# The opening of a two-layer mixer kernel: sum of squares on TensorE, one scaling instruction, earlier modulation loads, weight splits on GpSimd

## The chip, the cores and the metric

The kernel runs on one core of a Trainium2 chip. The metric is device time in microseconds (us) for one execution of the whole program; lower is better. The engines are called by the names of the profile: PE is TensorE's matrix product, PEld its weight load, DVE is VectorE, ACT is ScalarE, POOL is GpSimd, SP is SyncE, which issues the DMAs.

## What is computed

Two layers over 1024 latent tokens and 256 context tokens, each 1024 wide. The opening of the first layer is what the change touches:

```python
shift, scale, gate = jnp.split(jax.nn.silu(c) @ w_mod + b_mod, 3, axis=-1)
shift_c, scale_c, gate_c = jnp.split(jax.nn.silu(c_ctx) @ w_mod + b_mod, 3, axis=-1)
h = rms_norm(x, g_pre) * (1 + scale[:, None, :]) + shift[:, None, :]
hc = rms_norm(xc, g_pre) * (1 + scale_c) + shift_c
z = split_cols(h @ w_in)
zc = split_cols(hc @ w_in)
```

`rms_norm` divides by the root of the mean square over the 1024 channels and multiplies by a vector. The rest of the layer is four token mixers (pooling, latent attention, differential attention, windowed attention), gates, a merge and an output projection. All of it is float32.

## The kernel before

Tokens lie in the free dimension and channels in the partitions, so a chunk of 512 tokens is eight tiles (k = 0 to 7) of 128 x 512. There are three chunks: 0 and 1 are the latent tokens, 2 is the context (256 wide). To keep float32 accuracy on TensorE, each operand is split into a high half and a low half (`split`, line 66: ScalarE rounds to the high half, another engine subtracts), and one product becomes three instructions (`mm3`, lines 76 to 78).

`startup` (line 360) is the opening. Three weight tiles are applied to chunk 0 while it is being normalised: for each k, nine products (three tiles by three) go into three banks of PSUM. This is called group k here. What stands before and around it:

- `fetch` (line 376) loads x in four DMAs of 512 KB for a chunk. `st.load` (line 270) loads one weight tile of 512 KB (384 KB for the one of 96 columns) into `wraw`, of which there are two buffers, and splits it; in the opening the low half is made by VectorE (`nc.vector`), and by GpSimd elsewhere (the default). `mod_load` (line 408) loads two tiles of 512 KB of modulation weights, `wmod` (3 buffers) and `wmr` (6 buffers).
- `scaled` (line 384) is the norm of a chunk: `sum_sq` squares tile by tile on ScalarE and adds on VectorE or GpSimd, `col_rs` (line 232) sums over the partitions by products with a column of ones on TensorE, scales on VectorE and takes the power -1/2 on GpSimd; `spread` (line 247) makes a row for all partitions from that, by four diagonals on VectorE and four products on TensorE. For chunk 0 the row is copied to SBUF (`rbs`) and GpSimd multiplies it into the eight tiles.
- `mod_rows(k)` and `mod_run(k)` compute shift for the 128 channels of tile k on TensorE (line 422, a transpose at 430), and `scale_dot(k, i)` computes scale by a dot over 1024 elements on VectorE (line 150); i = 0 is for the latent tokens, i = 1 for the context. `silu_row(i)` makes the row that the dots use, by `spread`.
- `finish(k, ...)` applies scale and shift to tile k and makes its two halves. For chunk 0 that is two ScalarE passes and a VectorE subtraction, for the other chunks a VectorE instruction (line 56), a ScalarE pass and another VectorE instruction.

A planner reorders instructions between the program and the queues of the engines, by an estimate of when each is ready; the written order is its priority. Each queue then runs in order. The DMAs all go through SP's queue. When chunk 0 is through, `startup` finishes chunks 1 and 2, and their products follow with the same three weights.

Two buffers matter for the change: `h_tile(1, 1)`, 128 x 8 x 512, holds the low halves of chunk 1 and is not used until then, and the PSUM tiles `pt` (two) hold what `spread` returns.

Of the kernel before, what the change touches and what calls it, by code (L numbers as in the profile page):

```python
# [8 lines left out]
F = mybir.dt.float32  # L9
# [7 lines left out]
D = 1024  # L17
# [15 lines left out]
def kernel(ctx: ExitStack, tc: tile.TileContext, A: dict, out: bass.AP):  # L33
# [326 lines left out]
    def startup(es, three, crow):  # L360
# [10 lines left out]
        h_tile(1, 0)  # L371

# [9 lines left out]
        rbs = {}  # L382

# [10 lines left out]
        def finish(k, c0, n):  # L394
            c = 0 if c0 < SEQ else 1
            x, hi, lo = X(k, c0), H(0, k, c0, n), H(1, k, c0, n)
            a, b = m0.ab[:, 1, k, c:c + 1], m0.ab[:, 0, k, c:c + 1]
            if c0:
                stt(x, x, a, rbs[c0], ALU.mult, ALU.mult)
                act(hi, x, AF.Identity, bias=b)  # L400
                stt(lo, x, b, hi.bitcast(F), ALU.add, ALU.subtract)
            else:
                act(x, x, AF.Identity, scale=a, bias=b)
                split(x, hi, lo)
# [3 lines left out]
        def mod_load(k):  # L408
            if k < KT:
                mw[k] = p.tile([128, KT, 128], F, name="wmod", tag="wmod", bufs=3)  # L410
# [27 lines left out]
        fetch(*ALL[0])  # L438
        st.load((0, three[0]), None, nc.vector)
        mod_load(0)  # L440
        st.load((0, three[1]), None, nc.vector)
        mod_load(1)
        st.load((0, three[2]), tiles, nc.vector)
        mod_load(2)
        def silu_row(c):
            for g in range(2):
                act(crow[c][:, g * 512:g * 512 + 512], spread(cs[:, 4 * g:4 * g + 4, c], 512, p, sq1))
        silu_row(0)
        side = scaled(*ALL[0])
        next(side)  # L450
        mod_rows(0)
        next(side)
        mod_run(0)
        mod_rows(1)
        next(side)
        row = p.tile([128, 512], F, name="rbs", tag="nacc")
        act(row, rbs[0])
        for k in range(KT):
            x = X(k, 0)
            tt(x, x, row, ALU.mult, nc.gpsimd)  # L460
        big = ps_s.tile([128, 1536], F, name="pss", tag="pss")
        for k in range(KT):
            mod_load(k + 3)
            mod_run(k + 1)
            mod_rows(k + 2)
            finish(k, *ALL[0])
            for i, t in enumerate(three):
                m = 96 if t == W_X else 128
                st.group((0, t), big[0:m, i * 512:i * 512 + 512], 0, 512, [k])
            if k == 1:  # L470
                silu_row(1)
            if k > 1 and k < 8 - WMB + 2:
                scale_dot(k - 2, 1)
            if k < 4:
                fetch(*ALL[1], [2 * k])
            if k == 4:
# [1181 lines left out]
```

## Time and profile before

| what | us |
| --- | --- |
| median of 3 runs | 2758.21 (2756.69 to 2758.29) |
| the profiled execution, its own time | 2752.67 |
| its span in the trace | 2750.5 |
| TensorE busy in the span | 2615.1 (95%) |
| VectorE busy | 1539.2 (56%) |
| ScalarE busy | 1185.3 (43%) |
| GpSimd busy | 810.2 (29%) |
| mean granted TensorE clock | 0.977 |

A busy TensorE is not one at its peak, since ends of products are modelled and overlap; the granted clock tells which of its two levels (1.2 and 2.4 GHz) a stretch had. Times in the rows are counted from the start of the span.

### The profile page before, as it was taken

The page shows a single profiled execution, that of the slowest core. Times are in us where ns is not written, and L with a number is a line of the kernel's source. Part 1 is how long each engine was busy: PE and PEld are TensorE (multiplying, and loading weights), DVE is VectorE, ACT ScalarE, POOL GpSimd, SP SyncE. Part 2 cuts the span into 40 slices and gives each one's busy share as a digit, 9 for nine tenths or more (in the row PEclk, how much of TensorE's full clock was granted, in tenths as well). Part 3 has the DMA queues.
Part 4 walks back from the last instruction along what each step waited for, and adds up shares of the span by engine and source line. Part 5 has one row for each costly group of instructions (what it writes and reads, how often), then busy time and mean ns, then how long its engine had stood idle before and what let it go on. Part 6 is the DMA issues. An engine that isn't in the chain of part 4 may idle for free.

```text
span 2750.5 us, 38390 instructions
## 1 busy us (share of the span) xinstructions
PE 2615.1 (95%) x14194; PEld 2208.5 (80%) x14194; DVE 1539.2 (56%) x2638; ACT 1185.3 (43%) x2176; POOL 810.2 (29%) x492
## 2 busy tenths in 40 slices
PE   7998998999999989999998998989999999999998
PEld 5777877788988878888877776877888888888878
DVE  7544788967654893322148553889866632233133
ACT  4433765666662211222245343776656722222231
POOL 4223434300002223433324313445100022444334
PEclk9999999999999999999999999999999999999999
DMA  6366324323434652221135276434423343222122
GB/s 237 104 196 203 121 81 136 120 85 95 116 120 138 200 165 73 76 75 61 35 104 192 85 204 195 139 100 132 118 72 111 88 131 104 79 85 88 48 77 100
DMA packets 209069, 322.27 MB, mean 117 GB/s; under 512 B 26740, under 2 KB 123634, under 8 KB 208882
## 3 DMA queue, kind: packets, MB, share of 16 engines
q1 hardware_dynamic: 208882, 319.83, 37.4%
q8 instruction: 111, 1.82, 0.3%
q14 instruction: 76, 0.62, 0.1%
HBM read 239.07 MB, written 77.86 MB: 115 GB/s over the span
## 4 chain that ended last, share of the span: by engine, by line
PE 72%; DVE 14%; DMA 4%; issue 4%; ACT 3%; POOL 2%; SPq 1%; POOLq 0%; DVEq 0%; ACTq 0%
PE pd L76 14%; PE pd L78 14%; PE pd L77 14%; PE acc L1018 6%; PE pt L1002 5%; PE pss L1113 2%; PE pt L76 2%; PE pt L77 2%; PE pt L78 2%; DVE P L974 2%; DVE mjunk L150 2%; PE pss L1171 1%; PE pss L1072 1%; DVE t L53 1%; PE pss L1074 1%
## 5 line engine op out<-in xcount | busy, mean ns | idle before, releaser
L76 PE MATMUL pd<-h,wh 128*128 128x512 f32 (+2 forms) x2288 | 859.2, 376 | 22.2 <-ACT sg L50 10.5
L78 PE MATMUL pd<-h,wl 128*128 128x512 f32 (+2 forms) x2288 | 846.0, 370 | 0.2 <-POOL wl L53 0.2
L77 PE MATMUL pd<-h,wh 128*128 128x512 f32 (+2 forms) x2288 | 845.4, 370 | 0.2 <-DVE h L56 0.2
L53 POOL TENSOR_TENSOR wl<-wraw,wh 128x1024 fp32r<-128x1024 f32 x106 | 260.2, 2455 | 1009.8 <-ACT wh L50 801.7
L76 PEld LDWEIGHTS pd<-h,wh 128*128 128x128 f32 (+1 forms) x2288 | 437.7, 191 | 87.7 <-ACT sg L50 11.3
L78 PEld LDWEIGHTS pd<-h,wl 128*128 128x128 f32 (+1 forms) x2288 | 436.7, 191 | 68.9 <-issue 1.5
L77 PEld LDWEIGHTS pd<-h,wh 128*128 128x128 f32 (+1 forms) x2288 | 437.8, 191 | 60.1 <-DVE h L56 1.0
L974 DVE CUSTOM_DVE_ANT_0 P<-pss,zero 128x1280 f32<-128x1280 f32 (+1 forms) x216 | 295.6, 1369 | 118.1 <-PE pss L1113 60.4
L53 DVE TENSOR_TENSOR tl<-pt,th 128x512 fp32r<-128x512 f32 (+1 forms) x420 | 276.8, 671 | 114.0 <-ACT th L50 110.8
L50 ACT ACTIVATE th<-pt 128x512 fp32r<-128x512 f32 (+1 forms) x420 | 241.0, 583 | 182.3 <-PE pt L1002 174.9
L53 DVE TENSOR_TENSOR sg<-sg,pt 128x512 f32<-128x512 f32 x96 | 65.4, 686 | 394.7 <-PE pt L78 394.7
L1002 PE MATMUL pt<-kc,P 128*128 128x128 f32 x1632 | 255.8, 277 | 14.4 <-DVE P L56 8.8
L1018 PE MATMUL acc<-th,vt 128*128 128x256 f32 x816 | 245.3, 314 | 6.3 <-ACT th L50 5.8
L1018 PE MATMUL acc<-tl,vt 128*128 128x256 f32 x816 | 220.2, 290 | 6.5 <-DVE tl L53 6.5
L50 ACT ACTIVATE wh<-wraw 128x1024 fp32r<-128x1024 f32 x124 | 130.6, 1053 | 201.8 <-PE pd L77 153.7
L1002 PEld LDWEIGHTS pt<-kc,P 128*128 128x128 f32 x1632 | 193.7, 142 | 25.1 <-DVE P L56 13.8
L50 ACT ACTIVATE sg<-pd 128x512 f32<-128x512 f32 x128 | 75.7, 591 | 318.7 <-PE pd L78 312.4
L50 ACT ACTIVATE P<-P,m 128x1280 f32<-128x1280 f32 (+1 forms) x144 | 182.8, 1269 | 69.8 <-DVE m L974 67.7
L53 POOL TENSOR_TENSOR m<-m,sg 128x512 f32<-128x512 f32 x96 | 131.4, 1375 | 197.6 <-DVE sg L53 196.3
L1018 PEld LDWEIGHTS acc<-th,vt 128*128 128x128 f32 x816 | 156.5, 192 | 37.2 <-ACT th L50 23.4
L1018 PEld LDWEIGHTS acc<-tl,vt 128*128 128x128 f32 x816 | 156.9, 192 | 19.7 <-DVE tl L53 12.8
L50 ACT ACTIVATE P<-P,negm 128x1280 f32<-128x1280 f32 (+3 forms) x144 | 146.6, 1018 | 31.3 <-DVE negm L974 30.4
(290 smaller groups left out, 3950.6 us busy)
## 6 DMA issues: line engine op xcount, KB each, us to landing
wraw<-in_w_in_dram SPq DMA_DIRECT2D x108, 512.0 KB, 3.5
wmt<-in_w_modt_dram SPq DMA_DIRECT2D x64, 256.0 KB, 2.9
wraw<-in_w_out_dram SPq DMA_DIRECT2D x32, 512.0 KB, 3.3
yd<-ot SPq DMA_DIRECT2D x108, 128.0 KB, 1.9
kt<-dkd SPq DMA_DIRECT2D x64, 160.0 KB, 3.2
qt<-dqd SPq DMA_DIRECT2D x72, 128.0 KB, 2.8
ya<-yd SPq DMA_DIRECT2D x36, 256.0 KB, 3.0
yb<-yd SPq DMA_DIRECT2D x36, 256.0 KB, 3.0
```

Of the source, the lines that this page charges most:

```text
L50: return nc.scalar.activation(out=o, in_=i, func=func, **kw)
L53: return (e or nc.vector).tensor_tensor(out=o, in0=a, in1=b, op=op)
L76: nc.tensor.matmul(ps, wh(k), xh(k), start=k == 0, stop=False)
L77: nc.tensor.matmul(ps, wh(k), xl(k), start=False, stop=False)
L78: nc.tensor.matmul(ps, wl(k), xh(k), start=False, stop=k == n - 1)
L150: nc.vector.tensor_tensor_reduce(out=jk, in0=a, in1=b, scale=1.0, scalar=start, op0=ALU.mult, op1=ALU.add, accum_out=o)
L974: nc.vector.tensor_tensor_reduce(out=o, in0=i, in1=zero.to_broadcast([128, nk]) if mask is None else mask, scale=-1.0, scalar=1e30 if h is ...
L1002: t = nc.tensor.transpose(pt[:, 2 * j + i, :], Ps[i][:, (g + j) * 128:(g + j + 1) * 128], ident)
L1018: nc.tensor.matmul(acc, vt[:, kts[g + j], :], x[:, j, :], start=g + j == 0 and a == 0, stop=g + j == nk - 1 and a == 1)
L1072: nc.tensor.matmul(o, qt[0:96, 0, qs], kh[0:96, ks], start=True, stop=False)
L1074: nc.tensor.matmul(o, qt[0:96, 1, qs], kh[0:96, ks], start=False, stop=True)
L1113: last["s"] = nc.tensor.matmul(ps[:, b0 - k0:b0 - k0 + n], qt[:, mp, qs], kv[mp][:, b0:b0 + n], start=True, stop=True)
```

## The change

Five things are changed in `startup`:

- The sum of squares of chunk 0 is no longer added up tile by tile. `first_rs` squares each tile on ScalarE and sums it over the partitions on TensorE at once: four products of one column for each of eight tiles, 32 in all. One VectorE reduction adds the eight partial sums; scaling and power follow as before.
- `finish` for chunk 0 takes the form of the other chunks: one VectorE instruction multiplies x by scale and by the spread row, which stays in PSUM. The copy `rbs` and GpSimd's eight products go.
- Modulation loads 0 to 5 are issued before the loop, load 0 ahead of the first weight tile. Loads 3 to 6 get their `wmod` from the memory of `h_tile(1, 1)`. Loads 6 and 7 follow at k = 1 and 2, and after them, at k = 2, all of chunks 1 and 2 of x.
- The low halves of the three weight tiles are made by GpSimd (the default of `st.load`).
- `silu_row(1)` and the first two dots of the context move to k = 0 and 1, and `finish(k)` moves ahead of `mod_run(k + 1)` and `mod_rows(k + 2)`.

```diff
+        spare = h_tile(1, 1, F).rearrange("p k n -> p (k n)").rearrange("p (s k n) -> p s k n", s=4, k=KT)
...
+        def first_rs():
+            pc = ps_o.tile([128, 512], F, name="acc", tag="acc")
+            for k in range(KT):
+                q = p.tile([128, 512], F, name="sq", tag="sq", bufs=3)
+                act(q, X(k, 0), AF.Square)
+                for i in range(4):
+                    nc.tensor.matmul(pc[:, 4 * k + i:4 * k + i + 1], q[:, i * 128:(i + 1) * 128], ones[:, 0:1],
+                                     start=True, stop=True)
+            rs = p.tile([128, 4], F, name="crs", tag="crs")
+            nc.vector.tensor_reduce(out=rs, in_=pc[:, 0:32].rearrange("p (k i) -> p i k", i=4), axis=AX.X, op=ALU.add)
+            ts(rs, rs, 1.0 / D, EPS, ALU.mult, ALU.add)
+            tt(rs, rs, nhalf[:, 0:4], ALU.pow, nc.gpsimd)
+            return rs
...
-            if c0:
-                stt(x, x, a, rbs[c0], ALU.mult, ALU.mult)
-                act(hi, x, AF.Identity, bias=b)
-                stt(lo, x, b, hi.bitcast(F), ALU.add, ALU.subtract)
-            else:
-                act(x, x, AF.Identity, scale=a, bias=b)
-                split(x, hi, lo)
+            stt(x, x, a, rbs[c0], ALU.mult, ALU.mult)
+            act(hi, x, AF.Identity, bias=b)
+            stt(lo, x, b, hi.bitcast(F), ALU.add, ALU.subtract)
...
-                mw[k] = p.tile([128, KT, 128], F, name="wmod", tag="wmod", bufs=3)
+                own = k < 3 or k == 7
+                mw[k] = p.tile([128, KT, 128], F, name="wmod", tag="wmod", bufs=3) if own else spare[:, k - 3]
...
-        fetch(*ALL[0])
-        st.load((0, three[0]), None, nc.vector)
-        mod_load(0)
-        st.load((0, three[1]), None, nc.vector)
-        mod_load(1)
-        st.load((0, three[2]), tiles, nc.vector)
-        mod_load(2)
...
+        fetch(*ALL[0])
+        mod_load(0)
+        st.load((0, three[0]))
+        mod_load(1)
+        st.load((0, three[1]))
+        mod_load(2)
+        st.load((0, three[2]), tiles)
+        for k in range(3, 6):
+            mod_load(k)
         silu_row(0)
-        side = scaled(*ALL[0])
-        next(side)
+        rs0 = first_rs()
         mod_rows(0)
-        next(side)
+        mod_rows(1)
+        rbs[0] = spread(rs0, 512, p, sq1)
         mod_run(0)
-        mod_rows(1)
-        next(side)
-        row = p.tile([128, 512], F, name="rbs", tag="nacc")
-        act(row, rbs[0])
-        for k in range(KT):
-            x = X(k, 0)
-            tt(x, x, row, ALU.mult, nc.gpsimd)
         big = ps_s.tile([128, 1536], F, name="pss", tag="pss")
         for k in range(KT):
-            mod_load(k + 3)
+            if k in (1, 2):
+                mod_load(k + 5)
+            finish(k, *ALL[0])
             mod_run(k + 1)
             mod_rows(k + 2)
-            finish(k, *ALL[0])
             for i, t in enumerate(three):
                 m = 96 if t == W_X else 128
                 st.group((0, t), big[0:m, i * 512:i * 512 + 512], 0, 512, [k])
+            if k == 0:
+                silu_row(1)
+                scale_dot(0, 1)
             if k == 1:
-                silu_row(1)
-            if k > 1 and k < 8 - WMB + 2:
-                scale_dot(k - 2, 1)
-            if k < 4:
-                fetch(*ALL[1], [2 * k])
-            if k == 4:
+                scale_dot(1, 1)
+            if k == 2:
+                fetch(*ALL[1])
                 fetch(*ALL[2])
                 side = scaled(*ALL[1], nc.gpsimd)
```

## Rows read from the trace of the kernel before

**Rows 1.** The page: busy time, share of the span and instructions of each engine.

```profile
PE 2615.1 (95%) x14194; PEld 2208.5 (80%) x14194; DVE 1539.2 (56%) x2638; ACT 1185.3 (43%) x2176; POOL 810.2 (29%) x492
```

**Rows 2.** Busy time in windows of 5 us; columns as the first line says.

```profile
core 0: us, PE busy (x) PEld busy (x) DVE busy (x) ACT busy (x) POOL busy (x), PEclk, DMA share, GB/s
10.00:15.00 5.00, 2.27 (x11) 1.96 (x11) 2.33 (x4) 2.58 (x4) 0.00 (x0) 1.00 1.06 390
...
35.00:40.00 5.00, 5.00 (x29) 3.24 (x29) 3.40 (x10) 2.44 (x5) 0.00 (x0) 1.00 0.95 333
```

**Rows 3.** Timeline, 5 to 33 us: start, duration, engine, line, what, count, [idle before].

```profile
5.35 0.63 ACT L50 ACTIVATE nacc<-h 128x512 f32<-128x512 f32 x1 [2.29 <-DMA h<-in_xt_dram]
8.32 2.08 PE L254 MATMUL pt<-dg,sq 128*128 128x128 f32 x8 [2.54 <-DVE dg L62]
13.13 1.86 PE L236 MATMUL acc<-ones,nacc 128*128 128x1 f32 x8 [2.73 <-DVE nacc L53]
14.92 3.57 PE L422 MATMUL pd<-wmod,cs 128*2 128x128 f32 x16
15.03 0.16 DVE L64 TENSOR_SCALAR crs<-acc 128x4 f32<-128x4 f32 x1 [1.96 <-PE acc L236]
15.11 1.23 DVE L53 TENSOR_TENSOR wl<-wraw,wh 128x1024 fp32r<-128x1024 f32 x1
15.27 1.95 POOL L53 TENSOR_TENSOR crs<-crs,nhalf 128x4 f32<-128x4 f32 x1 [14.34 <-DMA wmod<-in_w_mods_dram]
20.41 1.16 PE L254 MATMUL pt<-dg,sq 128*128 128x128 f32 x8 [0.38 <-DVE dg L62]
20.74 12.06 POOL L53 TENSOR_TENSOR h<-h,rbs 128x512 f32<-128x512 f32 x8 [3.52 <-ACT rbs L50]
```

**Rows 4.** The same timeline around group 0, and the last product of group 7.

```profile
29.55 0.50 PE L76 MATMUL pss<-h,wh 128*128 128x512 f32 x1
29.83 1.04 ACT L50 ACTIVATE w<-wraw 128x1024 fp32r<-128x1024 f32 x1
31.92 1.97 DVE L53 TENSOR_TENSOR w<-wraw,w 128x1024 fp32r<-128x1024 f32 x1
31.95 1.91 PE L422 MATMUL pd<-wmod,cs 128*2 128x128 f32 x16
33.94 0.50 PE L78 MATMUL pss<-h,w 128*128 128x512 f32 x1
...
65.50 0.63 PE L78 MATMUL pss<-h,w 128*128 128x512 f32 x1
```

**Rows 5.** The same timeline: VectorE's dots, and its scaling by the row in PSUM.

```profile
42.95 1.21 DVE L150 CUSTOM_DVE_ANT_0 jk<-wmr,z 128x1024 f32<-128x1024 f32 x1
44.40 2.12 DVE L150 CUSTOM_DVE_ANT_0 jk<-wmr,z 128x1024 f32<-128x1024 f32 x1
...
75.09 2.06 DVE L56 SCALAR_TENSOR_TENSOR h<-h,ab,pt 128x512 f32<-128x512 f32 x3
```

**Rows 6.** Timeline and windows (columns as rows 2) in a run of one-column products.

```profile
89.11 2.27 PE L549 MATMUL pss<-ones,n 128*128 128x1 f32 x16
...
89.27:90.30 1.03, 1.03 (x13) 1.03 (x11) 0.00 (x0) 0.00 (x0) 0.00 (x0) 1.00 0.00 0
90.30:91.38 1.08, 1.08 (x7) 1.08 (x7) 0.00 (x0) 0.00 (x0) 0.00 (x0) 0.52 0.00 0
```

**Rows 7.** GpSimd's splits (count, sum, mean ns); SP's waits; weight loads on the page.

```profile
L53 POOL TENSOR_TENSOR wl<-wraw,wh 128x1024 fp32r<-128x1024 f32 x4 | 9.6, 2394 | 27.3 <-ACT wh L50 27.3
...
SPq L72 <- DVE wl L53: 5.6, 1, 5.6
...
wraw<-in_w_in_dram SPq DMA_DIRECT2D x108, 512.0 KB, 3.5
```

**Rows 8.** Timeline: chunk 1's last load, and its first scaled tiles.

```profile
41.25 0.43 SPq L72 DMA_DIRECT2D h<-in_xt_dram  x1
...
68.01 2.05 DVE L56 SCALAR_TENSOR_TENSOR h<-h,ab,pt 128x512 f32<-128x512 f32 x3
```

## The prediction

> **What bounds the kernel now.** I read the head of the page first: TensorE is busy for 95% of the 2750.5 us span [rows 1]. An edit to the opening can only pay where TensorE is not yet fed, so next came busy time in slices of 5 us: from 10 to 15 us TensorE works 2.27 us of five, from 35 us on all of them [rows 2]. The timeline of the first 21 us shows why: a single chain. The squares of the first chunk (ScalarE, about 0.63 us each, from 5.35 us) are added up by VectorE. Four column sums on TensorE follow (eight instructions at 13.13), then the scaling (15.03), the power on GpSimd (15.27, 1.95 us) and the spread of the result. From 20.74 GpSimd multiplies eight tiles, 12.06 us in all [rows 3].
>
> The first product of the projection starts at 29.55, but the start that counts is later. The third weight's low half is made by VectorE from 31.92 to 33.89, and the last three products of group 0 wait for it until 33.94. The last product of group 7 starts at 65.50 [rows 4]: (65.50 - 33.94) / 7 = 4.51 us a group. TensorE needs for one group nine products of 512 columns (0.21 us each at 2.4 GHz, the higher of its two levels), one run of modulation rows (sixteen instructions, 1.91 us [rows 4]) and a transpose with its gaps: some 4.2 us. So from group 1 on TensorE is nearly the bound, and only an earlier 33.94 pays.
>
> The written order is not the order of execution. The first modulation rows stand before the column sums in the program and run after them [rows 3]: a planner orders each engine's queue by its own estimate of readiness. I must infer that order for the new kernel.
>
> **Removed, and off the path.** Gone are seven VectorE additions, eight GpSimd products and, from each group, one of two ScalarE passes. VectorE gets one instruction more per group, in the form of line 56 with the spread row in PSUM (2.06 us for three, 0.69 each [rows 5]). Per group VectorE then has two of these, 1.38 us, a dot of 1.21 us [rows 5] and three small ones of about 0.5 us together: 3.1 us. TensorE's 4.2 us hide that; without that cover the added one would cost 8 x 0.69 = 5.5 us, and a dot beside GpSimd work can take 2.12 us [rows 5]. I count nothing for it, nor for moving silu_row(1): its spread was ready early and filled a wait at 20.41 [rows 3], and it can fill the wait before group 0 ends again; if not, its sixteen instructions cost TensorE twice the 1.16 us of that row.
>
> **Added: 32 column sums on TensorE.** Each is two weight loads of 128 columns and two products of one column, so 64 instructions stand where eight stood. Eight took 1.86 us at 13.13, though the clock column reads 1.00 [rows 2, 3]. Sixteen of the same form took 2.27 us at 89.11, and in the stretch of it with the granted clock at 1.00 thirteen instructions begin in 1.03 us [rows 6]. So the opening runs at the lower of TensorE's two levels (1.2 GHz) whatever the column says. The modulation rows agree (sixteen in 3.57 us at 14.92, 1.91 us at 31.95), and the spreads (eight in 2.08 us at 8.32, 1.16 at 20.41): the rise falls between 15 and 20 us, while the engine was in that run of 128-column products [rows 3, 4].
>
> By 3.57 / 16 the lower level costs 64 x 0.22 = 14.1 us; by 0.1 each the higher costs 6.4. Which holds? At 89.11 TensorE goes through one-column products without a gap, and the granted clock falls from 1.00 to 0.52 in the middle of them [rows 6]. A stream of this form did not hold the higher level, so I take it that it does not bring it either: 14.1 us. The squares come faster (0.63 us a tile, against 1.76 us of sums).
>
> The first square is done at 5.98; the second half of the first silu row (2.08 us at 8.32 [rows 3]) is still to run on TensorE. End of the sums: 5.98 + 2.0 + 14.1 = 22.1 us, against 13.13 + 1.86 = 14.99 before.
>
> The Trainium skill ("TensorE: Matmul & The Clock Gate", Part 1: The HAM clock gate) puts this the other way for unbroken work: "the default state is throttled, and activity releases the throttle". The trace agrees for the modulation rows, where the clock rose; whether one-column products are such activity decides between the two prices, and the fall after 89 us speaks against it. That reading is the first rival below.
>
> **The queue behind it.** The scaling takes 0.16 us [rows 3]. The reduction has no row: it reads 32 columns from PSUM, so it lies between nothing beyond that scaling and the 0.69 us of a 512-column instruction [rows 5]; I take 0.2, the nearer in size. Power on GpSimd, 1.95 us: 22.5 to 24.5. The weight splits are now in the same GpSimd queue, 2.39 us each [rows 7], and 1.8 for the 96-column one by its size; on VectorE they took 1.23 to 1.97 [rows 3, 4]. In the old order VectorE took the scaling (15.03) ahead of the first split (15.11) [rows 3], and now a further 1 MB of modulation weights is loaded ahead of that first weight. So I expect the planner to queue the power first and the splits behind it.
>
> The first split then runs from 24.5 to 26.9. The raw weights have two buffers, and the third load on SP waits for the first split, as it did before (5.6 us of wait on the VectorE split [rows 7]); now it is issued at 26.9, with modulation loads 3 to 7 stuck behind it, and chunk 1's loads behind those. To landing 3.5 us [rows 7] gives 30.4, the high half on ScalarE 1.04 us [rows 4] gives 31.4, the low half 33.8. Group 0 ends its wait at 33.8, against 33.9.
>
> The scaled tile itself is ready earlier: spread at 26.2 (behind modulation rows 0 on TensorE, 22.1 to 25.7), VectorE 0.7, ScalarE 0.7, and some hops: about 28.3, against 29.55 [rows 4]. If the planner puts the first split ahead of the power, this path decides. Nine products after 28.3 end by 30.5, modulation rows 2 (1.91) may stand between, and group 1 starts near 32 instead of 34: -2 us.
>
> **Chunk 1.** Its four loads now stand behind modulation load 7, which waits for the second dot with the context's silu row; before, three were out earlier and the last was issued at 41.25 [rows 8], landed near 45. From 26.9, the third weight (0.5 MB), modulation loads 3 to 7 (5.2 MB) and chunk 1 (2.1 MB) take 20 us at 390 GB/s [rows 2], so they land by 47. The first scaled tile of chunk 1 was at 68.01 [rows 8], after eight squares, GpSimd's sums and one more spread. A later start of the sums costs up to 2 us, and a first chunk without stalls (4.2 for 4.51 us a group, seven times) gives 2 back. I count zero, with +-2.
>
> **Sum.** Between -0.1 (power first) and -2 (split first), with chunk 1's +-2: I take -1.0 us. The profiled execution took 2752.67 us (2750.5 of span, 2.2 around it) and would take 2751.7; the runs' median is 5.5 above it, so 2757.2.
>
> **Rivals.**
> - *The clock rises during the sums.* At 0.1 us each they keep pace with the squares and end near 13. Power to 15.3, first split to 17.7, third weight issued 17.7, landed 21.2, split by 24.7: group 0 is through 9 us earlier, chunk 1's loads move up with it, and most of it, -8, passes on: 2750 (2749 to 2753). For: TensorE would work without a gap from 6 us on, as it did before the rise near 18. Against: the fall after 89 us [rows 6].
> - *GpSimd's queue becomes the bound, through one interleaving.* Modulation rows 0 need the first load behind x, which lands while the sums run. If the planner puts those sixteen instructions ahead of the last sums, the sums end 3.6 us later, at 25.7, and everything behind the power moves along: third weight split at 37.4, group 0 through +3.5 us later; splits and chunk 1's sums on GpSimd then stretch two or three of VectorE's dots by 0.9 us each [rows 5], +2: 2763 (2760 to 2766). It decides from the point where the last column sum ends after 22.2 us. For: the rows stand first among what is ready. Against: the old order, where the sums went first [rows 3].
>
> **How the numbers follow.** Forecast 0.50, earlier clock 0.32, interleaving 0.18. Two tenths of a per cent, about what a measurement of this kernel can tell from no change, are 5.5 us: faster needs under 2752.7, slower over 2763.7. Nearly all of the first rival lies below that, and a little of the forecast: faster 0.32. Of the second somewhat under half lies above, and a few points are for costs that I bounded too low: slower 0.14. Same 0.54. The range is 2749 to 2763, with both rivals' middles in or at it; the forecast's own is 2753.5 to 2760.
>
> **What would show it.** Right: 64 one-column instructions about 0.22 us apart from 6 to near 22 us; the power on GpSimd near 22.5; SP waiting some 10 us on a GpSimd split before the third weight; the last products of group 0 at 33 to 34; the first chunk's last product at 64 to 66. Wrong: instructions 0.1 us apart before 15 us, the third weight issued before 20, group 1 starting before 28 (first rival); modulation rows among the column sums and group 0 ending after 36 (second). It also falls if chunk 1's first scaled tile, and not group 0, sets the difference.

## The result, and the profile after

The changed kernel takes 2774.93 us (median of 4 runs, 2769.65 to 2777.11) against 2757.46 for the kernel before on the same chip (4 runs, 2756.69 to 2758.29): ratio 1.0058, 95% interval 1.0039 to 1.0077. It is slower by 17.5 us, outside the predicted range. The profiled execution of after took 2775.81 us, 23 more than that of before, whose own time lay some 5 us under its median. So places in the opening are compared below between traces, and totals by medians only.

If the j-th product (lines 76 to 78) from the end of one trace is set against the j-th from the end of the other, after is 12.2 us late where group 0 ends, 13 to 16 through groups 1 to 6, 17.4 where group 7 ends, 21.3 at chunk 1's start, up to 27 within chunk 1 and 22.8 at 108 us. From there to the end it is mostly 22 to 24 (21 to 27 at the extremes, 23 at the end). In this pair of traces all of the loss lies in the first 110 us, in two places. TensorE's share on the page is again 95%, with 18.9 us more of busy time than in [rows 1]:

```profile
PE 2634.0 (95%) x14250; PEld 2225.1 (80%) x14250; DVE 1532.8 (55%) x2637; ACT 1180.8 (43%) x2167; POOL 805.7 (29%) x487
```

The timeline of after from 6 to 29 us, all engines (columns as [rows 3]; line numbers are those of the changed file, where the column sums of chunk 0 are L391 and the modulation rows L434):

```profile
6.04 5.28 PE L391 MATMUL acc<-ones,sq 128*128 128x1 f32 x24 [0.32 <-ACT sq L50]
...
13.02 8.53 PE L391 MATMUL acc<-ones,sq 128*128 128x1 f32 x40
...
21.48 3.57 PE L434 MATMUL pd<-wmod,cs 128*2 128x128 f32 x16
21.59 0.19 DVE L394 TENSOR_REDUCE crs<-acc 128x4 f32<-128x32 f32 x1 [14.96 <-PE acc L391]
...
22.07 1.02 POOL L53 TENSOR_TENSOR crs<-crs,nhalf 128x4 f32<-128x4 f32 x1 [21.13 <-DVE crs L64]
...
25.10 0.27 ACT L50 ACTIVATE mrow<-pd 2x128 f32<-2x128 f32 x1 [7.93 <-PE pd L434]
25.27 1.04 ACT L50 ACTIVATE wh<-wraw 128x1024 fp32r<-128x1024 f32 x1
26.39 2.34 POOL L53 TENSOR_TENSOR wl<-wraw,wh 128x1024 fp32r<-128x1024 f32 x1 [3.29 <-ACT wh L50]
28.75 0.33 SPq L72 DMA_DIRECT2D wraw<-in_w_in_dram  x1
```

The 64 column sums (24, then the second half of the first silu row, then 40) take 0.21 to 0.22 us each and end at 21.55, where [rows 3] have 14.99. The power is through at 23.09. Then the split does not start: its input, the high half `wh`, is a ScalarE instruction that stands behind `mrow`, the copy of modulation rows 0, in ScalarE's queue. ScalarE is idle for 7.93 us until those rows leave TensorE, which does them after the column sums. The third weight's load, issued behind the split, goes out at 28.75. Group 0 of after, in the same view, against [rows 4]:

```profile
36.05 0.60 ACT L50 ACTIVATE z<-pt 128x512 f32<-128x512 f32 x1 [1.67 <-PE pt L254]
36.54 0.84 ACT L50 ACTIVATE wh<-wraw 128x768 fp32r<-128x768 f32 x1
37.45 1.82 POOL L53 TENSOR_TENSOR wl<-wraw,wh 128x768 fp32r<-128x768 f32 x1 [8.72 <-ACT wh L50]
...
39.33 0.47 PE L78 MATMUL pss<-h,wl 128*96 128x512 f32 x1 [1.01 <-POOL wl L53]
39.73 1.91 PE L434 MATMUL pd<-wmod,cs 128*2 128x128 f32 x16
...
41.73 0.27 ACT L50 ACTIVATE mrow<-pd 2x128 f32<-2x128 f32 x1 [2.64 <-PE pd L434]
41.91 1.04 ACT L50 ACTIVATE w<-wraw 128x1024 fp32r<-128x1024 f32 x1
43.02 3.02 POOL L53 TENSOR_TENSOR w<-wraw,w 128x1024 fp32r<-128x1024 f32 x1 [3.75 <-ACT w L50]
...
46.10 0.79 PE L78 MATMUL pss<-h,w 128*128 128x512 f32 x1 [1.85 <-POOL w L53]
```

The same happens twice more: the second high half stands behind a copy of the second silu row (36.05), the third behind the third `mrow` (41.73), each of which waits for TensorE. Group 0 ends at 46.10 in place of 33.94. From the start of the first split to the end of the third low half it takes 19.7 us (26.39 to 46.04). Before needed nearly as long, 18.8 us (15.11 to 33.89 [rows 3, 4]), so of the 12.2 us 11.3 are the later start of the first split. Then groups 2 to 5 follow at 4.28 us each (group 1 takes 6.66, group 6, which has no modulation rows, 2.44), and the second loss comes in group 7:

```profile
65.18 2.28 POOL L53 TENSOR_TENSOR nacc<-nacc,sq 128x512 f32<-128x512 f32 x1 [19.13 <-ACT sq L50]
67.89 14.99 POOL L53 TENSOR_TENSOR nacc<-nacc,sq 128x512 f32<-128x512 f32 x10 [0.43 <-ACT sq L50]
...
74.57 0.40 PE L78 MATMUL pss<-h,wl 128*128 128x512 f32 x1
78.90 1.87 PE L236 MATMUL acc<-ones,nacc 128*128 128x1 f32 x8 [3.94 <-POOL nacc L53]
...
82.86 0.63 PE L78 MATMUL pss<-h,w 128*128 128x512 f32 x1
86.33 1.01 PE L236 MATMUL acc<-ones,nacc 128*128 128x1 f32 x4 [2.84 <-POOL nacc L53]
...
89.29 2.06 DVE L56 SCALAR_TENSOR_TENSOR h<-h,ab,pt 128x512 f32<-128x512 f32 x3 [0.44 <-PE pt L254]
...
90.85 1.22 PE L76 MATMUL pd<-h,wh 128*128 128x512 f32 x2 [1.59 <-ACT h L50]
```

Chunk 1's squares are added by GpSimd from 65.18 on (from 41.21 in before), up to 2.3 us an addition. Its column sums (eight instructions of L236) stand in TensorE's queue in the middle of group 7 and wait for them; six products of group 7 wait behind. The same happens at 86.33 with the context's sums. Chunk 1's first scaled tile is at 89.29 in place of 68.01 [rows 8]. In the windows (columns as [rows 2]) TensorE, while it waits, falls to the lower clock and, with more waits in between, stays there for some 27 us (0.50 from 80 to 100 us, 0.82 in the ten after):

```profile
10.00:15.00 5.00, 5.00 (x25) 5.00 (x25) 0.00 (x0) 1.74 (x4) 0.00 (x0) 1.00 1.03 402
...
75.00:80.00 5.00, 1.10 (x6) 1.10 (x6) 1.40 (x2) 1.67 (x4) 4.77 (x5) 0.63 0.00 2
80.00:85.00 5.00, 3.48 (x10) 2.27 (x10) 2.59 (x7) 2.33 (x5) 4.76 (x6) 0.50 0.00 0
...
95.00:100.00 5.00, 5.00 (x21) 4.51 (x21) 5.00 (x9) 2.45 (x4) 0.00 (x0) 0.50 0.00 0
```

SP's waits in the first 50 us show both delays of loads, beside [rows 7]: the third weight waits 15.5 us for the GpSimd split, and modulation loads 6 and 7, with chunk 1's loads behind them, 10.4 us for VectorE's dots:

```profile
SPq L72 <- POOL wl L53: 15.5, 1, 15.5
SPq L72 <- DVE sums L150: 10.4, 2, 7.8
```

### The profile page after: what moved, and what is told of

Read it like the earlier page. It is cut to its first block, busy times and chain, and to the rows that moved or that the text cites. A ratio compares the mean times of both kernels' runs of the same rounds, so it can differ in the third digit from the quotient of the medians.

```text
span 2774.0 us, 38488 instructions
## 1 busy us (share of the span) xinstructions
PE 2634.0 (95%) x14250; PEld 2225.1 (80%) x14250; DVE 1532.8 (55%) x2637; ACT 1180.8 (43%) x2167; POOL 805.7 (29%) x487
## 4 chain that ended last, share of the span: by engine, by line
PE 74%; DVE 11%; issue 5%; DMA 4%; POOL 3%; ACT 2%; SPq 1%; POOLq 0%; DVEq 0%; ACTq 0%
PE pd L76 14%; PE pd L78 14%; PE pd L77 14%; PE acc L1027 7%; PE pt L1011 6%; PE pss L1122 3%; PE pt L76 2%; PE pt L77 2%; PE pt L78 2%; DVE mjunk L150 2%; DVE P L983 1%; PE pss L1180 1%; PE pss L1081 1%; PE pss L1083 1%; PE pss L1082 1%
## 5 line engine op out<-in xcount | busy, mean ns | idle before, releaser
L76 PE MATMUL pd<-h,wh 128*128 128x512 f32 (+2 forms) x2288 | 859.4, 376 | 25.1 <-ACT sg L50 10.4
L1011 PEld LDWEIGHTS pt<-kc,P 128*128 128x128 f32 x1632 | 194.7, 143 | 23.5 <-DVE P L56 12.2
```

Source lines behind the costliest of these rows:

```text
L76: nc.tensor.matmul(ps, wh(k), xh(k), start=k == 0, stop=False)
L1011: t = nc.tensor.transpose(pt[:, 2 * j + i, :], Ps[i][:, (g + j) * 128:(g + j + 1) * 128], ident)
```

## The experiments

The theory from the traces: (a) late sums, then high halves in ScalarE's queue behind TensorE's results, cost 12 us at group 0; (b) the squares' additions on GpSimd, waited for by column sums inside TensorE's queue, cost the rest. The rivals: the splits on GpSimd alone, the order of the loads alone, the lower clock alone. All ratios are to the kernel before, on the same chip, with 95% intervals; "chunk 1" is the start of chunk 1's first product (69.55 before, 90.85 after). The places are those of one trace for each run. Of after's variants, e3, e6, e9 and e13 are not told apart from after by their intervals, and e2 and e5 barely; for these the places are the evidence.

| run | median us | ratio | group 0 ends | group 7's last product | chunk 1 |
| --- | --- | --- | --- | --- | --- |
| before | 2757.46 | 1 | 33.94 | 65.50 | 69.55 |
| after | 2774.93 | 1.0058 (1.0039 to 1.0077) | 46.10 | 82.86 | 90.85 |
| e1 | 2761.42 | 1.0011 (0.9997 to 1.0025) | 35.20 | 71.86 | 79.84 |
| e2 | 2764.91 | 1.0026 (1.0013 to 1.0039) | 39.28 | 72.30 | 80.30 |
| e3 | 2770.76 | 1.0051 (1.0036 to 1.0067) | 41.89 | 69.33 | 84.03 |
| e4 | 2761.68 | 1.0024 (1.0009 to 1.0038) | 47.22 | 77.19 | 82.39 |
| e5 | 2763.11 | 1.0020 (1.0001 to 1.0040) | 36.82 | 73.06 | 77.88 |
| e6 | 2776.94 | 1.0066 (1.0044 to 1.0087) | 43.11 | 84.18 | 84.61 |
| e7 | 2757.21 | 0.9997 (0.9986 to 1.0009) | 30.42 | 68.33 | 68.76 |
| e8 | 2756.72 | 1.0000 (0.9987 to 1.0012) | 28.62 | 69.38 | 69.61 |
| e9 | 2771.79 | 1.0051 (1.0039 to 1.0063) | 45.17 | 79.73 | 86.19 |
| e10 | 2758.90 | 1.0008 (0.9997 to 1.0018) | 29.29 | 67.27 | 67.50 |
| e11 | 2755.19 | 0.9998 (0.9987 to 1.0008) | 29.38 | 66.43 | 66.67 |
| e12 | 2752.18 | 0.9983 (0.9974 to 0.9992) | 28.84 | 59.67 | 59.90 |
| e13 | 2770.66 | 1.0047 (1.0033 to 1.0062) | 45.46 | 76.42 | 76.65 |
| e14 | 2759.33 | 1.0005 (0.9994 to 1.0015) | 35.31 | 65.86 | 68.34 |
| e15 | 2756.67 | 0.9988 (0.9975 to 1.0001) | 29.37 | 60.30 | 64.15 |

**e1: after, chunk 0's sum on VectorE again.**

```diff
 def first_rs():
-    pc = ps_o.tile(...)            # 32 column sums, reduction
-    ...
+    acc = p.tile([128, 512], F, name="nacc", tag="nacc")
+    for k in range(KT):
+        sum_sq(acc, X(k, 0), k, p)
+    return col_rs(acc, 512, p)
```

> The changed kernel, with the first chunk's squares again added up by VectorE and summed by four products on TensorE; all else as changed. Three theories for the 17 us. Late sums: the 64 one-column instructions at the lower clock (end 21.5 us) hold everything behind them, so without them the sums end near 15, the last products of group 0 come 6 us sooner (40 instead of 46.1) and the time falls by 6 to 9 us, to about 2767. Queue order: the loads put modulation weights ahead of the first weight, so the planner files the weights' high halves on ScalarE behind copies that wait for TensorE; that order stays, so group 0 still ends after 40 and the time stays over 2765. Slow splits: GpSimd's splits alone cost it, so nothing moves by more than 2 us (2773 to 2777).

Measured 2761.42: 13.5 of the 17.5 us are back, more than any of the three theories gave. Timeline of e1, all engines:

```profile
16.94 1.04 ACT L50 ACTIVATE wh<-wraw 128x1024 fp32r<-128x1024 f32 x1
18.06 2.42 POOL L53 TENSOR_TENSOR wl<-wraw,wh 128x1024 fp32r<-128x1024 f32 x1 [1.82 <-ACT wh L50]
20.50 0.33 SPq L72 DMA_DIRECT2D wraw<-in_w_in_dram  x1
...
35.20 0.80 PE L78 MATMUL pss<-h,w 128*128 128x512 f32 x1 [1.85 <-POOL w L53]
...
67.90 1.87 PE L236 MATMUL acc<-ones,nacc 128*128 128x1 f32 x8 [3.94 <-POOL nacc L53]
```

The whole chain of high half, split and third load moves up by 8.3 us, group 0 by 10.9. The sums on TensorE start the first loss. The order in ScalarE's queue is still that of after (`mrow` at 16.77, then the high half), and group 0 ends 1.3 us after that of before: that order alone does not make the 12 us. The wait inside group 7 stays as long as in after, 3.94 us, and only comes earlier: the second loss is another matter.

**e2: after, the three splits on VectorE.**

```diff
-st.load((0, three[0]))
+st.load((0, three[0]), None, nc.vector)      # and the other two alike
```

> The changed kernel, with the three weights' low halves made by VectorE again; all else as changed. Slow splits: 2.3 to 3.0 us each on GpSimd was the loss, so the time returns to within 3 us of the kernel before (2755 to 2761). Late sums and queue order: the high halves on ScalarE come as late as in the changed kernel (25.3, 36.5 and 41.9 us), so only the difference of the splits returns, 1 to 4 us: 2771 to 2774.

Measured 2764.91, 10 us back, between what the theories gave; group 0 ends 6.8 us earlier than in after. The high half still starts at 25.13, behind the first `mrow`, so GpSimd is not what holds it. The gain comes in the two rounds of the queue that follow: from the first split to the third low half they take 11.8 us in place of 19.7. The splits themselves (0.95 to 1.22 us a weight against 1.82 to 3.02) make 3.8 of that. In after VectorE is also held beside the first GpSimd split: one diagonal for the second silu row takes 2.08 us, where four take 0.88 at 23.13. Timeline of after, VectorE and the products that wait for it:

```profile
26.73 2.08 DVE L62 TENSOR_SCALAR dg<-kc,cs 128x128 f32<-128x128 f32 x1
...
28.86 1.65 PE L254 MATMUL pt<-dg,sq 128*128 128x128 f32 x4 [1.81 <-DVE dg L62]
```

**e3: after, each weight loaded ahead of its modulation pair, as before.**

```diff
-mod_load(0); st.load((0, three[0]))
+st.load((0, three[0])); mod_load(0)          # three times
```

> The changed kernel, with each weight loaded ahead of its pair of modulation loads, as before the change; all else as changed, the sums on TensorE too. Queue order: the first high half on ScalarE stands behind the squares alone (near 17 to 18 us instead of 25.3), the second near 21 to 27 instead of 36.5; the first split follows the power on GpSimd at 23, the third weight is issued near 25.5 instead of 28.75, group 0 ends at 34 to 38 instead of 46.1 and the time falls by 8 to 12 us, to 2763 to 2767. Late sums: the sums end at 21.5 all the same, so the time falls by at most 4 us. Slow splits: no change beyond 2 us.

Measured 2770.76, about 4 us back in the median, which the intervals do not tell from nothing; the theory of the queue order had 8 to 12, that of the late sums at most 4. With the old order ScalarE has the first high half at 17.11, ahead of `mrow`, and the split still starts only at 23.11, behind the power in GpSimd's queue. So the swap of `wh` and `mrow` came from the load order, and putting it back returns less than earlier sums do: the power, which waits for the sums, still holds the first split, and the second and third high halves (33.41, 37.51) still stand behind copies that wait for TensorE.

**e4: the kernel before with the column sums on TensorE alone.**

```diff
 def scaled(c0, n, e=None):
+    if c0 == 0:
+        box = first_rs(); yield; yield
+        rbs[c0] = spread(box, n, p, sq1); yield; return
```

> The kernel before, with only the first chunk's sum of squares moved to TensorE (32 sums of one column, one reduction); loads, splits and scaling as before. Late sums: the sums end near 21.5 instead of 15.0, and power, spread and GpSimd's eight products follow 6 to 7 us later, so the first product comes near 35.5 and the time rises by 5 to 9 us, to 2763 to 2767. Queue order: this kernel keeps the old loads and the first high half ahead of the modulation copy, so the third weight's low half stays the bound of group 0 and the time rises by 0 to 4 us. Slow splits: no change beyond 2 us.

Measured 2761.68 (interval of the ratio 1.0009 to 1.0038): the sums alone cost 2.5 to 10 us. The power moves from 15.27 [rows 3] to 22.34, GpSimd's eight products end at 40.9, the first product starts at 38.35 and group 0 ends at 47.22. That is 13.3 us late in the trace, 12.1 of it still at 108 us, for some 4 us in the median: a place in the opening does not pass on in full to the total.

**e5: after with one 512-column product per squared tile** among the column sums, into an unused PSUM tile; its result is not used.

```diff
+    nc.tensor.matmul(wide[:, 0:512], sq1, q, start=True, stop=True)   # after the four of tile k
```

> The changed kernel plus one product of 512 columns for each of the eight squared tiles (sixteen TensorE instructions, 6.8 us at the lower clock, their result unused) among the column sums. It adds work to the path and tells apart what keeps the opening at the lower level. If products of many columns raise the clock and one-column ones don't: the steps of the column sums fall from 0.21 to about 0.1 us after the first few tiles, the sums end at 15 to 19 us in spite of the added work, and the time falls by 3 to 8 us. If the opening is at the lower level for its first 18 us whatever TensorE does, or if column sums take 0.21 us for a reason other than the clock: the steps stay, the sums end at 25 us or later, and the time rises by 3 to 7 us.

Timeline of e5, TensorE, the first three tiles' column sums (L392):

```profile
6.27 1.87 PE L392 MATMUL acc<-ones,sq 128*128 128x1 f32 x8 [0.48 <-ACT sq L50]
...
11.55 1.40 PE L392 MATMUL acc<-ones,sq 128*128 128x1 f32 x8
...
13.75 0.95 PE L392 MATMUL acc<-ones,sq 128*128 128x1 f32 x8
```

From 13.75 on each column sum steps by 0.12 us, as at the higher level, while after's keep 0.21 to the end. With the added work the sums end no earlier (23.5), but TensorE is at the higher level behind them, the first high half comes at 19.80 and its split at 20.92, ahead of the power, and 2763.11 us are measured, some 11 back. In after TensorE went through the column sums, with eight 128-column products of the silu row among them, from 6 to 21.5 us, and the lower level held; in e5, with a 512-column product behind each tile's sums, the higher one was there by 13.75. The run also says that late sums alone do not make the first loss: they end 2 us later than in after, and group 0 ends 9.3 us sooner. Both the level and the order of ScalarE's and GpSimd's queues changed, and e5 does not tell the two apart.

**e6: after with chunk 1 loaded before the loop.**

```diff
 for k in range(3, 6):
     mod_load(k)
+fetch(*ALL[1])                               # and not at k == 2
```

> The changed kernel, with chunk 1's four loads issued before the loop (behind modulation load 5) instead of at k = 2 behind modulation load 7. Two separate losses: besides group 0's 12 us, chunk 1's squares were filed late on ScalarE (from 64 us), so GpSimd's sums ended at 78.8 and TensorE stood in group 7 and ahead of chunk 1. With the loads early the squares are filed among groups 2 to 5, group 7 ends within 4 us of the end of its neighbours' pace (near 76 instead of 82.9), chunk 1's first product comes near 80 instead of 90.8, and the time falls by 6 to 10 us. One loss only (everything follows from group 0's lateness): chunk 1's first product stays within 3 us of 90, and so does the time.

Measured 2776.94, nothing back, where the theory of late loads had 6 to 10. Group 0 ends 3 us earlier, then TensorE waits 3.4 us for chunk 1's and 4.3 us for chunk 2's GpSimd sums, and group 7's last product is at 84.18. Late loads alone are not the second loss.

**e7: the kernel before with the one-instruction scaling alone.**

```diff
-row = p.tile(...); act(row, rbs[0])
-for k in range(KT):
-    tt(X(k, 0), X(k, 0), row, ALU.mult, nc.gpsimd)
```

and `finish` in one form for all chunks.

> The kernel before, with only the norm and scale of chunk 0 in one VectorE instruction from the spread row in PSUM (no copy of the row, no eight GpSimd products). By the sum of the prediction this part is hidden and gives little: group 0's wait ends at 33 to 34, time within 2 us. Queue order: without GpSimd's products the diagonals of the second silu row and the split of the second weight don't stretch on VectorE (4.2 and 2.0 us beside them), and the high halves come ahead of the wait for the row on ScalarE, so group 0 ends at 28 to 31 and the time falls by 2 to 6 us. Against: one more VectorE instruction a group, at most 5.5 us, if TensorE's work doesn't cover it.

Measured 2757.21, no difference. Group 0 ends 3.5 us earlier (30.42), and chunk 1's first product only 0.8 us earlier (68.76): the gain is given back between. Timeline of e7, GpSimd and TensorE:

```profile
55.96 4.01 POOL L53 TENSOR_TENSOR nacc<-nacc,sq 128x256 f32<-128x256 f32 x4 [2.32 <-ACT sq L50]
...
59.93 1.02 POOL L53 TENSOR_TENSOR crs<-crs,nhalf 128x4 f32<-128x4 f32 x1
...
61.88 1.99 PE L254 MATMUL pt<-dg,sq 128*128 128x128 f32 x8 [3.56 <-DVE dg L62]
```

Chunk 1's column sums do not wait here (57.37), but the power that follows them stands behind four of the context's additions in GpSimd's queue. TensorE waits 3.56 us for the diagonals behind that power, with all of group 7 still to do.

**e8: the parts of the change that pay at group 0:** scaling and early modulation loads kept, the sums and splits as before, chunk 1 loaded early (e1, e2, e3 and e6 together).

```diff
-rs0 = first_rs()          # column sums per tile on TensorE
+rs0 = first_rs()          # as in e1
-mod_load(0); st.load((0, three[0]))
+st.load((0, three[0]), None, nc.vector); mod_load(0)     # three times
+fetch(*ALL[1])            # ahead of the loop
```

> The changed kernel without its two costly parts: the sum of squares and the weight splits on VectorE and the loads of weights ahead of modulation weights, as before; the one-instruction scaling and the early modulation loads are kept, and chunk 1 is loaded before the loop. If the two losses are the column sums with their queue and the late load of chunk 1: sums end near 15, group 0 ends at 27 to 31 instead of 33.9, chunk 1's first product comes at 60 to 65 instead of 69.6, and the time falls below the kernel before by 4 to 9 us. If something else in the change costs (silu row and context dots moved into groups 0 and 1, early modulation loads): the time is at or above that of before.

Measured 2756.72, no difference, where the theory had chunk 1 at 60 to 65 and 4 to 9 us. It has the same shape: group 0 5.3 us earlier, chunk 1's first product at 69.61, as before. Timeline of e8, TensorE:

```profile
51.94 1.83 PE L236 MATMUL acc<-ones,nacc 128*128 128x1 f32 x8 [3.41 <-POOL nacc L53]
...
65.39 0.79 PE L236 MATMUL acc<-ones,nacc 128*128 128x1 f32 x4 [3.84 <-POOL nacc L53]
```

Ahead of group 6 TensorE waits 3.4 us for GpSimd's additions of chunk 1 (41.31 to 51.88), ahead of group 7 3.8 us for those of the context.

**e9: after, every other addition of chunk 1 on VectorE.**

```diff
-sum_sq(acc, X(k, c0), k, p, e)
+sum_sq(acc, X(k, c0), k, p, None if c0 == 512 and k % 2 == 0 else e)
```

> The changed kernel with one thing different: of chunk 1's seven additions of squares, three (every other one) go to VectorE, four stay on GpSimd. Theory (chunk 1's sums on GpSimd, waited for by the column sums that stand inside group 7 in TensorE's queue, are the second loss, on top of the 12 us at group 0): group 0 still ends near 46, group 7 ends near 76 to 78 in place of 82.9, chunk 1's first product starts at 79 to 84 in place of 90.9, and 2764 to 2770 us in place of 2775. Rival (GpSimd's sums only fill time that something else, the late start or VectorE's dots, fixes anyway; VectorE has now more to do): group 7 still ends after 81, 2773 to 2778.

Measured 2771.79, 3 back (within the noise), and group 7 at 79.73, between the two expectations. Three of the additions took 0.7 to 1.2 us on VectorE, but four stayed on GpSimd, and the column sums of L236 still stood in group 7, waiting 3.65 us. Half of a chain was not a clean test; e13 beside e6 is one.

**e10, e11: e8 with the same edit, and with all seven additions of chunk 1 on VectorE.**

```diff
-sum_sq(acc, X(k, c0), k, p, e)
+sum_sq(acc, X(k, c0), k, p, None if c0 == 512 and k % 2 == 0 else e)   # e10
+sum_sq(acc, X(k, c0), k, p, None if c0 == 512 else e)                  # e11
```

> The kernel of e8 (one-instruction norm and scale, modulation loads early, sums and splits of the opening on VectorE, chunk 1 loaded early) with three of chunk 1's seven additions on VectorE. Theory (e8's 5 us were given back at chunk 1's sums alone): TensorE no longer waits in groups 6 and 7, group 7 ends near 59 to 62 in place of 69.4, chunk 1's first product at 61 to 66 in place of 69.6, and 2749 to 2754 us. Rival (something else caps chunk 1, such as the modulation dots on VectorE or a later stage that has slack of its own): 2756 to 2758.

> The kernel of e8 with all seven of chunk 1's additions on VectorE. Theory (GpSimd's additions of over 1.3 us each are what is waited for): as e10 or up to 2 us better, 2748 to 2754, group 7 near 60. Rival (VectorE, which also does the dots and the scaling of the groups, becomes the bound of the groups' pace): groups slower than 4.28 us each, group 7 ends after 65, 2755 to 2760.

Measured 2758.90 and 2755.19, no difference from before, at or near the numbers of the rivals (2756 to 2758, 2755 to 2760), though not for their reason: groups 1 to 3 of e11 were no slower than after's (4.54, 4.28 and 4.28 us). Timeline of e11, TensorE:

```profile
50.05 0.95 PE L236 MATMUL acc<-ones,nacc 128*128 128x1 f32 x8
...
62.12 1.01 PE L236 MATMUL acc<-ones,nacc 128*128 128x1 f32 x4 [5.19 <-POOL nacc L53]
63.00 0.77 PE L76 MATMUL pss<-h,wh 128*128 128x512 f32 x1
```

Chunk 1's sums no longer wait (50.05). But next in the queue, ahead of all of group 7, stand the context's column sums, and they wait 5.19 us for GpSimd. The stall moved one chunk on.

**e12: e11 with the context's additions on VectorE too.**

```diff
-sum_sq(acc, X(k, c0), k, p, None if c0 == 512 else e)
+sum_sq(acc, X(k, c0), k, p)
```

> The kernel of e11 with chunk 2's additions of squares on VectorE too. In e11 group 7's first product stood behind chunk 2's column sums in TensorE's queue, which waited 5.2 us for GpSimd, and its high half behind chunk 2's squares on ScalarE. Theory (these in-order queues behind GpSimd's additions are what caps the opening): group 7 ends at 56 to 60 in place of 66.4, chunk 1's first product follows at once, and 2747 to 2752 us. Rival (VectorE is now the bound: it has 2.8 us more, at 7 additions of about 0.4): group 7 ends after 63, 2754 to 2758.

Measured 2752.18, ratio 0.9983 (0.9974 to 0.9992): faster than both kernels, 5 us below before. Timeline of e12, TensorE, the same two groups of instructions:

```profile
49.51 0.95 PE L236 MATMUL acc<-ones,nacc 128*128 128x1 f32 x8
...
62.67 0.50 PE L236 MATMUL acc<-ones,nacc 128*128 128x1 f32 x4
```

Neither waits; the context's now stand behind group 7, whose last product is at 59.67. VectorE had room for the 14 additions.

**e13: after with chunk 1 loaded early and all additions of chunks 1 and 2 on VectorE;** chunk 0's sums stay on TensorE, the splits on GpSimd.

```diff
+fetch(*ALL[1])            # ahead of the loop, and not at k == 2
-sum_sq(acc, X(k, c0), k, p, e)
+sum_sq(acc, X(k, c0), k, p)
```

> The changed kernel with chunk 1 loaded before the loop, as in e6, and with the additions of squares of chunks 1 and 2 on VectorE. The sums of chunk 0 stay on TensorE, the splits on GpSimd. Theory (two losses: the 12 us at group 0, which stay, and the column sums that wait for GpSimd, which go): group 0 ends at 43 to 46, group 7 at 73 to 77, chunk 1's first product at 74 to 78, and 2762 to 2767 us. Rival (the second loss has another cause, such as the lower clock or VectorE's dots): group 7 ends after 80, 2771 to 2777.

Group 0 (45.46), group 7 (76.42) and chunk 1 (76.65) fell where the theory put them: without GpSimd's additions, the only difference from e6, the second loss is gone up to chunk 1 (e6 has 84.61), and from group 0 to chunk 1 the delay shrinks from 11.5 to 7.1 us. The total did not follow: 2770.66, above the expected 2767. The delay grows again behind chunk 1, to 15 us at 108 us and at 127. Timeline of e13, TensorE:

```profile
96.19 0.38 PE L76 MATMUL pd<-h,wh 128*128 128x256 f32 x1 [1.18 <-ACT n L50]
...
98.49 0.58 PE L76 MATMUL pd<-h,wh 128*128 128x256 f32 x1 [0.89 <-ACT h L50]
```

and its window from 100 us (columns as [rows 2]):

```profile
100.00:110.00 10.00, 10.00 (x49) 10.00 (x48) 2.29 (x3) 2.44 (x6) 2.55 (x2) 0.50 0.01 2
```

Chunk 2's scaled tiles come late, TensorE waits in the middle of that chunk, and the following ten microseconds run at the lower clock (and most of the ten after, 0.57), where before has 1.00. e12 has the first of these waits too (79.43, 1.18 us), with 0.66 in the one window from 85 to 90 us and 1.00 around it. So the wait need not bring the long stretch, and that the stretch is all of the further 8 us was read from these rows, not tested.

**e14 and e15: the kernel before with the additions of chunks 1 and 2 on VectorE; and the same with e7's scaling.**

```diff
-sum_sq(acc, X(k, c0), k, p, e)
+sum_sq(acc, X(k, c0), k, p)
```

> The kernel before with the additions of squares of chunks 1 and 2 on VectorE and nothing else. Theory (in the kernel before, group 0 at 33.9 and the groups' own pace set chunk 1's start, with GpSimd's sums close behind): group 7 ends at 64 to 66, chunk 1's first product at 65 to 69, 2754 to 2758 us. Rival (the moved sums alone make e12's gain): 2750 to 2753.

> e14 with the one-instruction scaling of e7. Theory (e7's 3.5 us were taken back by chunk 1's sums on GpSimd alone): group 7 ends 3 to 4 us ahead of e14's, and the time is 2 to 4 us below e14's, 2750 to 2755. Rival (something else caps chunk 1, such as VectorE or the loads): within 1 us of e14.

Measured 2759.33 and 2756.67. Moving the additions alone gives nothing (1.0005), and chunk 1 comes 1.2 us earlier. With the scaling, group 7's last product comes 5.6 us ahead of e14's and chunk 1 4.2 us, where e7 without the move kept 0.8; the time is 2.7 us below e14's, but neither is told apart from before. Both traces drift in stages far behind the opening that no edit touches: e15's is 3 us ahead of before's at 200 us and 7 behind at the end, e14's 4.7 and 6.6 behind. So a total here is good to a few microseconds, and the places in the opening tell more.

## Why the prediction was wrong, point by point

- **The sums: right.** Predicted 64 instructions 0.22 us apart, ending at 22.1; measured 0.21 to 0.22 and 21.55. Neither rival came: the clock did not rise in them, and the modulation rows stood behind the last sum (21.48), not ahead of it. The level rose early only in e5, where wide products stood among them.
- **Reduction and scaling: right** (0.19 and 0.17 us for 0.2 and 0.16). The power was queued ahead of the splits, as inferred, and took 1.02 us, not 1.95.
- **"The first split then runs from 24.5 to 26.9": the step that failed first.** I followed GpSimd's queue and took its input for ready. The high half is a ScalarE instruction, and the edit that I had named for the order of GpSimd's queue (a modulation load ahead of the weight) also turned the order on ScalarE: `mrow`, which needs TensorE, came ahead of `wh`. The first split ran at 26.39 to 28.73, only 1.8 us later than predicted, so little of the error is here.
- **"To landing 3.5 us gives 30.4, the high half on ScalarE 1.04 us gives 31.4, the low half 33.8": this is where 12.2 us went.** I had the first split 9.4 us later than in before and expected no delay from it, since I gave 9.3 us to the stretch from its start to the third low half; the rows of before have 18.8 for it [rows 3, 4], and after took 19.7. I counted one pass of that chain. There were three, since each high half on ScalarE stood behind a result of TensorE (rows 0, silu row 1, rows 2), and TensorE's own queue waited for the splits before it (39.33, 1.01 us for the second low half). The third weight's low half ended at 46.04, not 33.8. I had priced silu_row(1) at nothing on TensorE and had not asked what its copy holds up on ScalarE. The Trainium skill ("Perfetto Trace Analysis", "Tensor Engine Instruction (MATMUL, LD_WEIGHTS)") says that the queues of ScalarE, VectorE and GpSimd run strictly in order; the rows at 25.10 and 25.27, 36.05 and 36.54, 41.73 and 41.91 agree. I did use that of GpSimd's queue, and not of the engine in front of it. e1, e2 and e3 each take away one member of that chain and return 10.9, 6.8 and 4.2 us at group 0. How the loss divides among late sums, queue order, split engine and clock stays open: the shares depend on each other.
- **"I count zero, with +-2" for chunk 1: the step that failed second,** by 10.6 us (22.8 less 12.2) in the trace. I bounded when the loads land and not who waits for the sums. I had named chunk 1's additions on GpSimd, but only as a stretch of VectorE's dots (in the second rival). The column sums that read them stand in TensorE's queue inside group 7, so the wait holds up group 7 too, and the lower clock that follows holds for some 27 us. How much of the 10.6 is wait and how much clock was not tested. e6 and e9 left these waits and returned 0 and 3 us; e11 moved them on by one chunk; e12 and e13 removed them, and group 7 ran through.
- **"Only an earlier 33.94 pays": half right.** In e7 and e8 it came 3.5 and 5.3 us earlier and paid nothing, because of GpSimd's additions for chunks 1 and 2: in e8 the column sums waited for them, in e7 the power behind them in GpSimd's queue. e15, which is e7 without them, has chunk 1 4.6 us earlier than e7. What set chunk 1's start was the later of two chains, and I worked out one; the prediction's last sentence named this as what would make it fall. The other half of the argument, TensorE's 4.2 us a group against 4.51, was misread too. Only five of groups 1 to 7 have a run of modulation rows; e3's seven took 27.4 us against 31.6 in before, so there were some 4 us to give and not 2.
- **The range** had its upper end from one interleaving of 3.6 us. Every bound was that of one instruction or one wait; none was for a queue order that repeats itself per weight tile.

Some of the sums do not close to the microsecond: the two profiled executions differ by 23 us and the medians by 17.5, and the parts returned one at a time (13.5, 10, 4) add up to more than the whole, since each takes away a member of the same chain.

## What to carry to other kernels

When an instruction is moved to another engine, follow its inputs too, through the queue of the engine that makes them, and ask of each thing filed ahead of it there which engine it waits for: here three weight splits stood behind small copies that waited for TensorE, and a first split that started 11.3 us late ended group 0 12.2 us late. A reduction for the next chunk that is read by the busiest engine belongs to that engine's path, however idle the one that makes it; moving 14 additions from GpSimd to VectorE made the difference between a gain given back (e8) and one kept (e12, group 7 9.7 us earlier, some 5 us in the total, though the two intervals overlap a little). Before forecasting a gain from an earlier start, find the second chain that ends just behind the first.

## What the runs showed of the hardware

- The last 40 of the 64 one-column products with weight loads of 128 columns, without a gap from 13.02 to 21.55, stayed at 0.21 us each, the lower level, although the clock column reads 1.00 for that stretch (window 10:15 of after). With a 512-column product after every eight they went from 0.23 to 0.12 us each within 8 us (e5). The Trainium skill ("TensorE: Matmul & The Clock Gate", Part 1: The HAM clock gate) has it that activity releases the throttle. In after it was not released while those 40 ran, and the spread behind modulation rows 0 (eight products in 1.19 us at 24.99, against 2.06 at 11.18) was the first at the higher level.
- The power of 128 x 4 elements on GpSimd took 1.02 us in after, e1 (1.03) and e4, where VectorE did nothing beside it, and 1.95 in before [rows 3] and e12, where VectorE made a split at the same time. A GpSimd split of 128 x 1024 took 2.34 us in e5 with VectorE idle (20.92) and 3.02 beside a dot and two scalings on VectorE (43.02 of after). VectorE is held as well: one diagonal of 128 x 128 took 2.08 us beside a GpSimd split (26.73 of after), where four took 0.88 at 23.13.
